# Gate and up products by Strassen's recurrence in a two-layer encoder

## The chip, the core and the metric

The kernel runs on one core of a Trainium2 chip. The metric is the device time of one execution in microseconds (us). The core's engines are TensorE (PE in the rows, its weight loads PEld), VectorE (DVE), ScalarE (ACT), GpSimd (POOL) and SyncE (SP), which issues transfers. Each has a queue of its own and works through it in order; they wait for each other by semaphores. On TensorE the rows give the granted clock as a share of 2.4 GHz.

## The reference

The input is a sequence of 512 tokens of 1024 features, float32. Each of two layers computes, with `rmsnorm(x) = x * rsqrt(mean(x*x) + 1e-6) * gain`:

```
x = x + 0.5 * (silu(h @ w_gate) * (h @ w_up)) @ w_down     h = rmsnorm(x), inner width 2816
p = rmsnorm(x) @ w_in;  A, B, C = three attentions on parts of p
x = x + concat(A, B, C) @ w_out
x = x + 0.5 * (silu(h @ w_gate) * (h @ w_up)) @ w_down     with weights of its own
```

and a last rmsnorm follows. So there are four feed-forward blocks (two per layer) and two mixing stages. The change is in the feed-forward blocks.

## The kernel before

Activations lie transposed: features on the 128 partitions, the 512 tokens along the row. A vector of 1024 features is 8 chunks of [128, 512].

**Products.** Float32 products are made of three products of a rounded format. Each operand is split into a high half, a copy rounded by a cast on ScalarE, and a low half, operand minus high half by one subtraction on VectorE. `mm3` (L450) issues high by high, high by low and low by high, all summed in one PSUM bank. Weights come from memory in float32 (`wr`), and are split in the kernel into `wh` and `wl`; activations are `xgh` and `xgl` (L480).

**A gate/up step.** `ffn` (L673) takes the inner width in two halves of 11 steps, each of 128 inner features. A step is the product of the gate weights (8 chunks of the contraction, so 8 times 3 matmuls of 512 columns) and that of the up weights: 48 matmuls. `gate_steps` (L649) then multiplies by the norm's factor `nm.r`, applies silu, multiplies by the up product and splits the result into `hh` and `hl`. After 11 steps come 8 down products (`dn`) of 33 matmuls each, added to the residual `x` (`down_steps`, L664). There are 4 blocks of 2 halves, so 88 steps.

**Weight stream.** `advance` (L426) loads blocks of 512 KB up to three ahead and splits one ahead, each on three buffers of its own kind (`wraw`, `whi`, `wlo`). All loads are issued by SyncE.

**Residual.** The 8 chunks of `x` stay in the on-chip memory through a feed-forward block; they are stored to DRAM (`xd`) only before a mixing stage, and read back at its output products (`po`).

**The norm.** As chunk m of the new residual is ready, `norm_chunk` (L460) makes `xgh`, `xgl` and the chunk's squares; GpSimd adds the squares up, and two matmuls (`ssq`) and a short chain give `nm.r`. The last chunk's three matmuls of each product are moved to the end of a step, so that the other 42 can run before it is there.

**What sets the order.** The Python code records all operations, and `Recorder.schedule` (L223) lists them by priority (order in the code), readiness by its own costs (`cost`, L152), and free buffers. The result is a fixed order for each engine, with fixed buffers. All operations are issued in L345, so the rows below are told apart by tile names.

Of the kernel before, what the change touches and what calls it, by code (L numbers as in the profile page):

```python
# [18 lines left out]
P = 128  # L19
# [7 lines left out]
HJ = NJ // 2  # L27
EPS = 1e-6
# [105 lines left out]
class Recorder:  # L134
# [17 lines left out]
    def cost(self, eng, what, args, kw, out):  # L152

        n = out.free() if isinstance(out, View) else 1
        psum = any(isinstance(a, View) and a.base.pool == "psum" for a in args[1:])
        if eng == "PE":
            if what == "transpose":
                return 107, 60
            return (n / 2.4) * (4 if args[1].base.dtype == F32 else 1) + 2.5, 60
# [11 lines left out]
        if eng == "POOL":  # L171
            return (120 + 1.08 * n if what == "tensor_scalar" else 145 + 2.11 * n), 60
        return max(650, out.shape[0] * 4 * n / 360), 2000
# [188 lines left out]
class Kern:  # L362
# [18 lines left out]

    def bigt(self, s, shape, dt=F32):
        return self.nc.tile("big", shape, dt, s)
# [24 lines left out]

    def stream(self, blocks):
        self.blocks = blocks  # L410
        self.loaded = {}
        self.halves = {}
        self.nload = self.nsplit = 1
        self.nget = 0
        shape = list(blocks[0].shape)
        t = self.nc.tile("wraw", shape, F32, "wr")
        hi, lo = self.nc.tile("whi", shape, F32R, "wh"), self.nc.tile("wlo", shape, F32R, "wl")
        self.halves[0] = (hi, lo)

        def part(c):  # L420
            self.nc.sync.dma_start(t[:, c], blocks[0][:, c])
            self.nc.scalar.copy(hi[:, c], t[:, c])
            self.nc.vector.tensor_tensor(lo[:, c], t[:, c], hi[:, c].bitcast(F32), ALU.subtract)
        return part

    def advance(self, ahead=1):  # L426
        nc = self.nc
        while self.nload < len(self.blocks) and self.nload < self.nget + 3:
            src = self.blocks[self.nload]
            t = nc.tile("wraw", list(src.shape), F32, "wr")  # L430
            nc.sync.dma_start(t, src)
            self.loaded[self.nload] = t
            self.nload += 1
        while self.nsplit < self.nload and self.nsplit < self.nget + 1 + ahead:
            t = self.loaded.pop(self.nsplit)
            hi = nc.tile("whi", list(t.shape), F32R, "wh")
            lo = nc.tile("wlo", list(t.shape), F32R, "wl")
            nc.scalar.copy(hi, t)
            (nc.gpsimd if self.nsplit in self.slow else nc.vector).tensor_tensor(lo, t, hi.bitcast(F32), ALU.subtract)
            self.halves[self.nsplit] = (hi, lo)  # L440
            self.nsplit += 1

    def weight(self, ahead=1):
        self.advance(ahead)
        w = self.halves.pop(self.nget)
        self.nget += 1
        return w


    def mm3(self, ps, a, b, first, last):  # L450
        mm = self.nc.tensor.matmul
# [8 lines left out]
    def norm_chunk(self, nm, src, gain, last):  # L460
        nc = self.nc
        lo = None
        if gain is not None:
# [23 lines left out]
    def new_norm(self, dim=D, table=False):  # L487
        nm = Kern.Norm()
        nm.xg, nm.acc, nm.r, nm.rc, nm.dim, nm.table = [], None, None, None, dim, table
        return nm  # L490
# [24 lines left out]
    def split_steps(self, src, s, scale=None, eng=None):  # L515
        hi, lo = self.pair(s)
# [26 lines left out]
    def setup(self, blocks):  # L543
        nc, io = self.nc, self.io
        self.x = [self.slot("x") for _ in range(KD)]
# [6 lines left out]
        nm = self.new_norm(table=True)  # L552
        part = self.stream(blocks)
        part(slice(0, 2))
        for k in range(KD):
            nc.sync.dma_start(self.x[k], io["xT"][:, k, :])
            if k == 0:
                nc.sync.dma_start(self.gains, io["gains"])
            self.norm_split(nm, self.x[k], self.gains_cols(G_F1, k))()
            if k == 0:  # L560
                part(slice(2, KD))
        cst = nc.tile("keep", [P, NCONST], F32, "cst")
# [7 lines left out]
        for k in range(KD):  # L570
            self.start(self.norm_chunk(nm, self.x[k], None, k == KD - 1))
# [59 lines left out]
    def ffn_blocks(self, l, f):  # L631
        out = []
        for h in range(2):
            for j in range(HJ):
                for g in range(2):
                    out.append(self.io["wgu"][l, f, h * HJ + j, :, g])
# [12 lines left out]
    def gate_steps(self, nm, pss, hi, lo):  # L649
        nc = self.nc  # L650
        while nm.r is None:
            yield
        t = self.slot("t1")
        nc.vector.tensor_tensor(t, pss[0], nm.r, ALU.mult)
# [3 lines left out]
        nc.vector.tensor_tensor(t, pss[1], t, ALU.mult)  # L658
# [5 lines left out]
    def down_steps(self, nm, m, ps, after):  # L664
# [3 lines left out]
        nc.vector.tensor_tensor(self.x[m], self.x[m], t, ALU.add)  # L668
        yield
        if after:  # L670
            yield from after(m)

    def ffn(self, nm, after, task=None, final=None):  # L673
        for half in range(2):
# [3 lines left out]
            for j in range(HJ):  # L678
                if j == 1 and task and half == 0:
                    self.start(slowly(task, 6))  # L680
                w = [self.weight()]
                pss = [self.ps("gu"), self.ps("gu")]
                self.product(pss[0], w[0], nm.xg, range(KD - 1), 0, KD - 1)
                w.append(self.weight())
                self.product(pss[1], w[1], nm.xg, range(KD - 1), 0, KD - 1)
                for g in range(2):
                    self.product(pss[g], w[g], nm.xg, [KD - 1], 0, KD - 1)
                self.start(self.gate_steps(nm, pss, *h[j]))
            if half == 1:
                nm.xg = None  # L690
            for m in range(KD):
                if final and half == 1 and m == KD - 1:
                    final(h)
# [5 lines left out]
                self.start(self.down_steps(nm, m, ps, after if half == 1 else None))  # L699
# [153 lines left out]
    def mix(self, l, nm, after):  # L853
# [233 lines left out]
        def post(u):  # L1087
# [18 lines left out]
            mixed[k] = yield from self.split_steps(o, "mx", eng=None if kind == "c" else nc.gpsimd)  # L1106
# [81 lines left out]
    def run(self):  # L1188
        nc, g = self.nc, self.gains_cols
        blocks = []  # L1190
        self.slow = set()
        for l in range(DEPTH):
# [6 lines left out]
        def follow(base, table, store=False):  # L1199
            nxt = self.new_norm(table=table)  # L1200

            def after(m):
                if store:
                    nc.sync.dma_start(self.xd[m], self.x[m])
                yield from self.norm_chunk(nxt, self.x[m], None if base is None else g(base, m), m == KD - 1)
                if store:
                    self.x[m] = None
            return nxt, after

        for l in range(DEPTH):  # L1210
            nxt, after = follow(G_MIX + 8 * l, True, True)
            self.ffn(nm, after, self.setup_all() if l == 0 else None)
            nm = nxt
            nxt, after = follow(G_F2 + 8 * l, False)
            self.mix(l, nm, after)
            nm = nxt
            if l + 1 < DEPTH:
                nxt, after = follow(G_F1 + 8 * (l + 1), True)
                self.ffn(nm, after)
# [3 lines left out]
    def finale(self, nm):  # L1223
# [62 lines left out]
        self.ffn(nm, after, final=final)  # L1286
# [5 lines left out]
T = {'offs': (1, 3, 5, 6), 'fill': (3, 3, 3, 2, 2, 2, 1), 'v': 18, 'pairs': (22, 32, 40), 'tl': 1, 'po': 2, 'grp': 2, 'yst': 2, 'pool': (4, 5, 11, 17, 19, 21, 23, 25), 'cstt': 3, 'psc': 0, 'order': (0, 6, 1, 3, 7, 4, 2, 5)}  # L1292
SIZES = {'slots': 57, 'big': 6, 'wraw': 3, 'whi': 3, 'wlo': 3, 'psum': 8, 'small': 24}
# [90 lines left out]
```

## Time and profile before

| | |
|---|---|
| time, median of 3 runs | 2028.42 us (2026.98 to 2028.52) |
| the profiled execution's own time | 2028.95 us, of which the span is 2027.1 us |
| TensorE busy | 1989.6 us (98%) |
| VectorE, ScalarE, GpSimd busy | 1088.9, 819.7, 371.3 us |
| TensorE's granted clock, mean | 0.989 of 2.4 GHz |
| moved by transfers | 231.35 MB, 114 GB/s |

A matmul's end is modelled, and matmuls overlap, so a busy share of TensorE says that it had something in it; its pace is read from the distance of starts. "Idle before" an operation names who released it. "To landing" is from the issue of a transfer to its last byte.

### The profile page before, as it was taken

The page shows a single profiled execution, that of the slowest core. Times are in us where ns is not written, and L with a number is a line of the kernel's source. Part 1 is how long each engine was busy: PE and PEld are TensorE (multiplying, and loading weights), DVE is VectorE, ACT ScalarE, POOL GpSimd, SP SyncE. Part 2 cuts the span into 40 slices and gives each one's busy share as a digit, 9 for nine tenths or more (in the row PEclk, how much of TensorE's full clock was granted, in tenths as well). Part 3 has the DMA queues.
Part 4 walks back from the last instruction along what each step waited for, and adds up shares of the span by engine and source line. Part 5 has one row for each costly group of instructions (what it writes and reads, how often), then busy time and mean ns, then how long its engine had stood idle before and what let it go on. Part 6 is the DMA issues. An engine that isn't in the chain of part 4 may idle for free.

```text
span 2027.1 us, 24516 instructions
## 1 busy us (share of the span) xinstructions
PE 1989.6 (98%) x9119; PEld 1644.0 (81%) x9119; DVE 1088.9 (54%) x1697; ACT 819.7 (40%) x1333; POOL 371.3 (18%) x322
## 2 busy tenths in 40 slices
PE   7999999999899999999999999999989999999997
PEld 5888888887688888888888888888867888888886
DVE  8444444579984434344543444356899744343435
ACT  5222223467784322222332222244668743222333
POOL 4100000146573000000100000012575620000001
PEclk8999999999899999999999999999999999999999
DMA  5434423574532223332323232245743332233222
GB/s 188 139 119 144 136 86 110 161 205 139 129 114 75 92 86 94 104 104 81 107 94 104 86 111 84 91 134 163 227 122 87 99 103 88 87 107 104 95 89 77
DMA packets 90247, 231.35 MB, mean 114 GB/s; under 512 B 12433, under 2 KB 14993, under 8 KB 90129
## 3 DMA queue, kind: packets, MB, share of 16 engines
q1 hardware_dynamic: 90128, 229.79, 36.5%
q8 instruction: 72, 1.18, 0.2%
q14 instruction: 47, 0.38, 0.1%
HBM read 197.24 MB, written 11.53 MB: 103 GB/s over the span
## 4 chain that ended last, share of the span: by engine, by line
PE 87%; DVE 7%; ACT 2%; issue 2%; POOL 1%; DMA 1%; SPq 0%; DVEq 0%; ACTq 0%; POOLq 0%
PE gu L345 47%; PE dn L345 24%; PE po L345 4%; PE pj L345 3%; PE pv L345 3%; PE sc L345 2%; PE av L345 2%; PE tr L345 2%; DVE p L345 1%; PE qn L345 1%; DVE wl L345 1%; ACT p L345 1%; POOL p L345 1%; DVE xgl L345 1%; DVE ptl L345 1%
## 5 line engine op out<-in xcount | busy, mean ns | idle before, releaser
L345 ACT CAST wh<-wr 128x1024 fp32r<-128x1024 f32 (+4 forms) x367 | 339.8, 948 | 857.8 <-PE gu L345 524.2
L345 PE MATMUL gu<-xgh,wh 128*128 128x512 f32 x1408 | 550.5, 391 | 1.7 <-ACT xgh L345 1.7
L345 PE MATMUL gu<-xgl,wh 128*128 128x512 f32 x1408 | 550.7, 391 | 1.1 <-DVE xgl L345 1.0
L345 PE MATMUL gu<-xgh,wl 128*128 128x512 f32 x1408 | 550.3, 391 | 1.2 <-DVE wl L345 1.2
L345 DVE TENSOR_TENSOR wl<-wr,wh 128x1024 fp32r<-128x1024 f32 (+4 forms) x351 | 389.5, 1129 | 139.5 <-ACT wh L345 139.0
L345 PEld LDWEIGHTS gu<-xgl,wh 128*128 128x128 f32 x1408 | 265.6, 189 | 58.1 <-DVE xgl L345 3.0
L345 DVE TENSOR_TENSOR t<-gu,r 128x512 f32<-128x512 f32 x88 | 60.8, 691 | 468.8 <-PE gu L345 468.8
L345 PEld LDWEIGHTS gu<-xgh,wh 128*128 128x128 f32 x1408 | 265.8, 189 | 57.7 <-ACT xgh L345 2.2
L345 PEld LDWEIGHTS gu<-xgh,wl 128*128 128x128 f32 x1408 | 265.6, 189 | 56.7 <-DVE wl L345 1.7
L345 POOL TENSOR_TENSOR sq<-sq,sq 128x512 f32<-128x512 f32 x52 | 79.9, 1536 | 1255.5 <-ACT sq L345 1250.1
L345 PE MATMUL dn<-hl,wh 128*128 128x512 f32 (+2 forms) x715 | 276.2, 386 | 0.0
L345 PE MATMUL dn<-hh,wl 128*128 128x512 f32 (+2 forms) x715 | 276.0, 386 | 0.0
L345 PE MATMUL dn<-hh,wh 128*128 128x512 f32 (+2 forms) x715 | 276.0, 386 | 0.0
L345 PEld LDWEIGHTS dn<-hh,wl 128*128 128x128 f32 x715 | 134.3, 188 | 27.1
L345 PEld LDWEIGHTS dn<-hh,wh 128*128 128x128 f32 x715 | 134.3, 188 | 27.1
L345 PEld LDWEIGHTS dn<-hl,wh 128*128 128x128 f32 x715 | 134.3, 188 | 27.0
L345 POOL TENSOR_SCALAR p<-p,ri 128x512 f32<-128x512 f32 x148 | 114.0, 779 | 95.0 <-DVE ri L345 66.2
L345 DVE SCALAR_TENSOR_TENSOR dt<-dn,r 128x512 f32<-128x512 f32 (+1 forms) x65 | 44.4, 683 | 115.9 <-PE dn L345 115.9
L345 ACT CAST hh<-t 128x512 fp32r<-128x512 f32 x88 | 54.7, 622 | 128.1 <-DVE t L345 128.1
L345 DVE TENSOR_TENSOR hl<-t,hh 128x512 fp32r<-128x512 f32 x88 | 62.0, 704 | 58.5 <-ACT hh L345 58.5
L345 DVE TENSOR_TENSOR ptl<-tr,pth 128x512 fp32r<-128x512 f32 x128 | 86.7, 681 | 8.3 <-ACT pth L345 7.7
L345 PE MATMUL tr<-cst,p 128*128 128x128 f32 x512 | 79.4, 279 | 8.3 <-DVE ptl L345 4.3
(190 smaller groups left out, 2476.5 us busy)
## 6 DMA issues: line engine op xcount, KB each, us to landing
wr<-in_wgu_dram SPq DMA_DIRECT2D x175, 512.0 KB, 3.9
wr<-in_wdn_dram SPq DMA_DIRECT2D x64, 384.0 KB, 3.1
wr<-in_wdn_dram SPq DMA_DIRECT2D x64, 320.0 KB, 3.1
wr<-in_wf_dram SPq DMA_DIRECT2D x26, 512.0 KB, 4.1
bias<-nd SPq DMA_DIRECT2D x32, 256.0 KB, 4.0
bias<-ba SPq DMA_DIRECT2D x32, 256.0 KB, 3.6
wr<-in_wo_dram SPq DMA_DIRECT2D x16, 512.0 KB, 3.7
bi<-in_lncm_dram SPq DMA_DIRECT2D x16, 256.0 KB, 4.6
```

Of the source, the lines that this page charges most:

```text
L345: o.fn(*[real(a) for a in o.args], **{k: real(a) for k, a in o.kw.items()})
```

## The change

**Recurrence.** For a step, the weights are seen as 2x2 blocks: rows are the two halves of the contraction (4 chunks each), columns are gate and up. The activations are 2x2 blocks too: the same halves by left and right 256 tokens. Seven products replace eight, each of 4 chunks by 3 matmuls of 256 columns: 84 matmuls for 48 of 512 columns. This holds for 86 of the 88 steps; the first two steps of the first block stay as they were (`T["plain"] = 2`).

**Sums of weights.** A step's weights come in four pieces. `a` is a block and a sum, `b` a sum and a block, `c` a sum and a block, `d` one sum. The sums in `a` and `c` are made by a load and a second transfer that adds to what lies there (`accum_op`), which GpSimd issues after the load has landed: 2 a step, 172 in all. Those in `b` and `d` are made by VectorE.

**Sums of activations.** `norm_fold` makes the differences `t12` and `t34` of the normed chunks on VectorE and splits them as well.

**Combining.** `gate_up` runs the seven products in three PSUM banks. After four of them a copy on ScalarE or an addition on VectorE must read a bank before TensorE may go on writing it.

**Buffers.** The nine weight buffers become a pool of 13 (`duo`), which also holds some pairs of the mixing stage; the general slots go from 57 to 49. The residual lies in DRAM throughout: `ffn` loads each chunk two down products ahead and stores it after the first half.

```diff
+    def load_piece(self, n):
...
+        if kind == "a":
+            nc.sync.dma_start(t[:, 0], b[0])
+            nc.sync.dma_start(t[:, 1], b[2])
+            nc.gpsimd.dma_start(t[:, 1], b[0], accum_op=ALU.add)
+        elif kind == "b":
+            nc.sync.dma_start(t[:, 1], b[3])
+        else:
+            nc.sync.dma_start(t[:, 0], b[2])
+            nc.gpsimd.dma_start(t[:, 0], b[3], accum_op=ALU.add)
+            nc.sync.dma_start(t[:, 1], b[1])
...
+    def split_piece(self, n):
...
+        if kind == "b":
+            nc.vector.tensor_tensor(t[:, 0], self.raw[n + 1][:, 0], self.raw[n - 1][:, 0], ALU.add)
+        elif kind == "d":
+            t = self.duo("wr", (P, 1, HD, P), F32)
+            nc.vector.tensor_tensor(t[:, 0], self.raw[n - 2][:, 0], self.raw[n - 1][:, 1], ALU.add)
+        hi, lo = self.duo("wh", t.shape), self.duo("wl", t.shape)
+        nc.scalar.copy(hi, t)
+        (nc.gpsimd if kind == "slow" else nc.vector).tensor_tensor(lo, t, hi.bitcast(F32), ALU.subtract)
...
+    def norm_fold(self, nm, src, gain, m):
...
+        nc.vector.scalar_tensor_tensor(t[:, right], g[:, right], -1.0, t[:, left], ALU.mult, ALU.subtract)
+        nc.vector.tensor_tensor(t34[:, left], g[:, right], g1[:, right], ALU.subtract)
+        nc.vector.scalar_tensor_tensor(t34[:, right], t[:, right], -1.0, g[:, left], ALU.mult, ALU.subtract)
+        h2, l2 = fac["T2"]
+        nc.scalar.copy(h2, t[:, right])
+        h, l = self.pair("t34")
+        nc.scalar.copy(h, t34)
...
+    def gate_up(self, nm, hi, lo):
...
+        self.folded(r1, w, 0, nm, "11", True)
+        nc.scalar.copy(s1[:, left], r1[:, left])
+        self.folded(r7, w, 1, nm, "T3", True)
+        nc.scalar.copy(s1[:, right], r7[:, left])
+        w = self.weight()
+        self.folded(r1, w, 0, nm, "T2", False)
+        nc.scalar.copy(s2[:, left], r1[:, left])
+        self.folded(r7, w, 1, nm, "T4", False)
+        nc.vector.tensor_tensor(u[:, left], r7[:, left], s2[:, left], ALU.add)
+        w = self.weight()
+        self.folded(r1, w, 0, nm, "T1", False)
+        nc.vector.tensor_tensor(u[:, right], r1[:, left], s1[:, right], ALU.add)
+        self.folded(r2, w, 1, nm, "21", True)
+        nc.vector.tensor_tensor(t[:, left], r2[:, left], s1[:, left], ALU.add)
+        w = self.weight()
+        self.folded(r1, w, 0, nm, "22", False)
+        self.start(self.gate_steps(nm, r1, t, u, hi, lo))
...
+    def ffn(self, nm, xs, after, task=None, final=None):
...
-                if j == 1 and task and half == 0:
+                if j == 4 and task and half == 0:
                     self.start(slowly(task, 6))
...
+            def load_x(m):
+                if m < KD:
+                    x[m] = self.slot("x")
+                    nc.sync.dma_start(x[m], xs[m])
...
-T = {'offs': (1, 3, 5, 6), 'fill': (3, 3, 3, 2, 2, 2, 1), 'v': 18, 'pairs': (22, 32, 40), 'tl': 1, 'po': 2, 'grp': 2, 'yst': 2, 'pool': (4, 5, 11, 17, 19, 21, 23, 25), 'cstt': 3, 'psc': 0, 'order': (0, 6, 1, 3, 7, 4, 2, 5)}
+T = {'plain': 2, 'load': 6, 'split': 2, 'offs': (1, 3, 5, 6), 'fill': (3, 3, 3, 2, 2, 2, 1), 'v': 18, 'pairs': (22, 32, 40), 'tl': 1, 'po': 2, 'grp': 2, 'yst': 2, 'pool': (4, 5, 11, 17, 19, 21, 23, 25), 'cstt': 3, 'psc': 0, 'order': (0, 6, 1, 3, 7, 4, 2, 5)}
-SIZES = {'slots': 57, 'big': 6, 'wraw': 3, 'whi': 3, 'wlo': 3, 'psum': 8, 'small': 24}
+SIZES = {'slots': 49, 'duo': 13, 'big': 6, 'psum': 8, 'small': 24}
```

**Where the order moves.** Two places, both in the second half of layer 0's second feed-forward block. First TensorE, before: the border of the gate and the up product of one step (`gu_1641` gate, `gu_1642` up).

```order
L345 MATMUL gu_1641_7693<-xgh_1380_5954,wh_1636_7628 128x512
L345 MATMUL gu_1641_7693<-xgl_1381_5966,wh_1636_7628 128x512
L345 MATMUL gu_1641_7693<-xgh_1380_5954,wl_1637_7639 128x512
L345 MATMUL gu_1642_7729<-xgh_1335_5734,wh_1639_7686 128x512 [waits Activation_49]
L345 MATMUL gu_1642_7729<-xgl_1336_5746,wh_1639_7686 128x512
L345 MATMUL gu_1642_7729<-xgh_1335_5734,wl_1640_7698 128x512 [waits DVE_49]
```

TensorE after: the border of the products "T3" (into `gu_2081`) and "T2" (into `gu_2080`, which holds "11" already).

```order
L349 MATMUL gu_2081_10297<-t34h_1664_7520,wh_2075_10118 128x256
L349 MATMUL gu_2081_10297<-t34l_1665_7534,wh_2075_10118 128x256
L349 MATMUL gu_2081_10297<-t34h_1664_7520,wl_2076_10219 128x256
L349 MATMUL gu_2080_10278<-t12h_1572_7125,wh_2078_10250 128x256 [waits Activation_49]
L349 MATMUL gu_2080_10278<-t12l_1573_7134,wh_2078_10250 128x256
L349 MATMUL gu_2080_10278<-t12h_1572_7125,wl_2079_10264 128x256 [waits DVE_49]
```

Before, the waits are for the new weights' halves. After, the wait on ScalarE is also for the copy `s1` out of `gu_2080`, and such a border comes every 12 matmuls. Second ScalarE, before:

```order
L345 CAST wh_1630_7618<-wr_1626_7513 128x1024 [waits DMAHW2_49,PE_49,Activation_49]
L345 CAST wh_1636_7628<-wr_1629_7573 128x1024 [waits DMAHW3_49,PE_49,Activation_49]
L345 ACTIVATE t1_1634_7621<-t1_1634_7621 128x512 [waits DVE_49]
L345 CAST hh_1561_7516<-t1_1634_7621 128x512 [waits DVE_49]
L345 CAST wh_1639_7686<-wr_1635_7583 128x1024 [waits DMAHW4_49,PE_49,Activation_49]
L345 CAST wh_1645_7696<-wr_1638_7641 128x1024 [waits DMAHW5_49,PE_49,Activation_49]
```

ScalarE after, in the step whose "11" and "T3" stand above (`DMASW` is a transfer that GpSimd issued):

```order
L349 CAST wh_2094_10261<-wr_2077_10150 128x1024 [waits DMAHW0_49,DMASW6_49,PE_49]
L349 COPY s1_2083_10300<-gu_2080_10278 128x256 [waits PE_49]
L349 ACTIVATE t1_2067_10275<-t1_2067_10275 128x512 [waits DVE_49]
L349 CAST wh_2107_10316<-wr_2090_10227 128x1024 [waits DMAHW4_49,DMASW7_49,PE_49]
L349 COPY s1_2083_10300<-gu_2081_10297 128x256 [waits PE_49]
L349 CAST wh_2092_10333<-wr_2091_10320 128x512 [waits DVE_49,Activation_49]
L349 COPY s2_2084_10340<-gu_2080_10278 128x256 [waits PE_49]
L349 CAST hh_1939_10081<-t1_2067_10275 128x512 [waits DVE_49]
```

Before, no cast stands in front of anything that TensorE needs within the step. After, the casts of summed pieces stand between the copies that free PSUM for TensorE: the cast `wh_2107` is ahead of the copy of `gu_2081`.

## Rows read from the trace of the kernel before

**Rows 1.** The page's head: span, then busy us, share of the span, instructions.

```profile
span 2027.1 us, 24516 instructions
PE 1989.6 (98%) x9119; PEld 1644.0 (81%) x9119; DVE 1088.9 (54%) x1697; ACT 819.7 (40%) x1333; POOL 371.3 (18%) x322
```

**Rows 2.** Chain that ended last, in order of time: start us, us, what.

```profile
203.45 119.68 PE gu L345 x528
323.13 59.84 PE dn L345 x264
...
1018.87 8.85 PE gu L345 x39
1027.71 0.47 PE ssq L345 x2
```

**Rows 3.** Timeline, TensorE, matmuls of 256 columns: start us, us, operation.

```profile
399.74 0.28 PE L345 MATMUL pv<-wh,xgh 128*128 128x256 f32 x1
...
406.10 0.28 PE L345 MATMUL pv<-wh,xgl 128*128 128x256 f32 x1
```

**Rows 4.** Stretches: busy us and count of PE, PEld, DVE, ACT, POOL; clock; DMA share; GB/s.

```profile
841.00:958.00 117.00, 117.00 (x518) 96.91 (x517) 44.11 (x51) 31.32 (x40) 0.00 (x0) 1.00 0.28 89
383.00:659.00 276.00, 269.02 (x1364) 222.35 (x1363) 218.35 (x448) 183.14 (x370) 146.05 (x131) 0.98 0.46 135
1378.00:1654.00 276.00, 268.33 (x1368) 222.32 (x1367) 218.53 (x449) 183.69 (x371) 146.73 (x131) 0.98 0.46 135
```

**Rows 5.** Groups by shape, VectorE: count, busy us, mean ns, idle before.

```profile
L345 DVE TENSOR_TENSOR wl<-wr,wh 128x1024 fp32r<-128x1024 f32 x209 | 259.2, 1267 | 39.9 <-ACT wh L345 39.4
L345 DVE TENSOR_TENSOR hl<-t,hh 128x512 fp32r<-128x512 f32 x88 | 62.0, 704 | 58.5 <-ACT hh L345 58.5
```

**Rows 6.** Timeline, VectorE, at the start and at the end of a down stage.

```profile
3.82 0.42 DVE L345 TENSOR_TENSOR wl<-wr,wh 128x256 fp32r<-128x256 f32 x1 [2.43 <-ACT wh L345]
18.92 5.42 DVE L345 TENSOR_TENSOR wl<-wr,wh 128x1024 fp32r<-128x1024 f32 x3
...
831.90 0.69 DVE L345 SCALAR_TENSOR_TENSOR dt<-dn,r 128x512 f32<-128x512 f32 x1 [2.04 <-PE dn L345]
832.63 0.69 DVE L345 TENSOR_TENSOR x<-x,dt 128x512 f32<-128x512 f32 x1
833.24 1.22 DVE L345 TENSOR_TENSOR wl<-wr,wh 128x1024 fp32r<-128x1024 f32 x1
```

**Rows 7.** ScalarE: groups by shape, and a 256-column cast from the timeline.

```profile
L345 ACT CAST wh<-wr 128x1024 fp32r<-128x1024 f32 x225 | 229.5, 1050 | 574.2 <-PE gu L345 472.7 <-PE dn L345 47.2 <-issue 36.1
L345 ACT CAST hh<-t 128x512 fp32r<-128x512 f32 x88 | 54.7, 622 | 128.1 <-DVE t L345 128.1
3.38 0.40 ACT L345 CAST wh<-wr 128x256 fp32r<-128x256 f32 x1 [1.37 <-DMA wr<-in_wgu_dram]
```

**Rows 8.** Landing of weight loads at 840:958 (512 KB), 781:839 (mostly 320/384 KB); two issues.

```profile
DMA to landing us min/median/max: 3.2/3.8/5.3
DMA to landing us min/median/max: 2.8/3.1/4.1
x<-xd SPq DMA_DIRECT2D x16, 256.0 KB, 4.5
wr<-in_wf_dram SPq DMA_DIRECT2D x26, 512.0 KB, 4.1
```

**Rows 9.** GpSimd, groups by shape: a two-input operation of 512 columns.

```profile
L345 POOL TENSOR_TENSOR p<-p,p 128x512 f32<-128x512 f32 x20 | 28.0, 1399 | 1.3
```

**Rows 10.** Timeline where the last output product gives the last residual chunk.

```profile
658.93 0.39 PE L345 MATMUL po<-mxh,wl 128*128 128x512 f32 x1
...
659.36 0.69 DVE L345 TENSOR_TENSOR x<-x,po 128x512 f32<-128x512 f32 x1 [2.65 <-PE po L345]
...
660.13 0.72 ACT L345 ACTIVATE xgh<-x,gains 128x512 fp32r<-128x512 f32 x1
```

**Rows 11.** Timeline at the start: what TensorE waits for.

```profile
34.30 0.80 PE L345 MATMUL ssq<-ssl,rep 128*128 128x512 f32 x1 [5.89 <-DVE ssl L345]
```

More of the change, by code (lines that the diff above doesn't have):

```diff
@@ L424, in stream @@
-        return part
-    def advance(self, ahead=1):
[L427 to L432, printed above, removed]
-            self.nload += 1
[L434 to L440, printed above, removed]
+        self.pieces = []
@@ new lines, in stream @@
+        for n, b in enumerate(blocks):
+            if isinstance(b, tuple):
+                b = [b[1][:, i // 2, HD * (i % 2):HD * (i % 2) + HD] for i in range(4)]
+                self.pieces += [(kind, b) for kind in "abcd"]
+            else:
+                self.pieces.append(("slow" if n in self.slow else "", b))
+        self.raw = {}
+        self.halves = {}
+        self.nload = self.nsplit = self.nget = 0
+    def load_piece(self, n):
+        nc = self.nc
+        kind, b = self.pieces[n]
+        if kind in ("", "slow"):
+            t = self.duo("wr", b.shape, F32)
+            nc.sync.dma_start(t, b)
+            return t
+        if kind == "d":
+            return None
+        t = self.duo("wr", (P, 2, HD, P), F32)
+        if kind == "a":
[4 more added lines that the diff above has]
+            nc.sync.dma_start(t[:, 1], b[3])
+        else:
+            nc.sync.dma_start(t[:, 0], b[2])
+            nc.gpsimd.dma_start(t[:, 0], b[3], accum_op=ALU.add)
+            nc.sync.dma_start(t[:, 1], b[1])
+        return t
@@ new lines, in split_piece @@
+    def split_piece(self, n):
+        nc = self.nc
+        kind = self.pieces[n][0]
+        t = self.raw[n]
+        if kind == "b":
[6 more added lines that the diff above has]
+        (nc.gpsimd if kind == "slow" else nc.vector).tensor_tensor(lo, t, hi.bitcast(F32), ALU.subtract)
+        self.halves[n] = (hi, lo)
@@ new lines, in advance @@
+    def advance(self, ahead=1):
+        while self.nload < len(self.pieces) and self.nload < self.nget + T["load"]:
+            self.raw[self.nload] = self.load_piece(self.nload)
+            self.nload += 1
+        fold = self.pieces[min(self.nget, len(self.pieces) - 1)][0] in "abcd" and self.pieces[self.nget][0]
+        while self.nsplit < self.nload and self.nsplit < self.nget + 1 + (T["split"] if fold else ahead):
+            if self.pieces[self.nsplit][0] == "b" and self.nload < self.nsplit + 2:
+                break
+            if self.nsplit not in self.halves:
+                self.split_piece(self.nsplit)
@@ L445, in weight, with mm3 @@
         w = self.halves.pop(self.nget)
+        self.raw.pop(self.nget - 3, None)
         self.nget += 1
         return w
-    def mm3(self, ps, a, b, first, last):
-        mm = self.nc.tensor.matmul
+    def mm3(self, ps, a, b, first, last, **kw):
+        mm = partial(self.nc.tensor.matmul, **kw)
         mm(ps, a[0], b[0], start=first, stop=False)
@@ L462, in norm_chunk @@
         lo = None
-        if gain is not None:
+        if gain is not None and nm.fold:
+            self.start(self.norm_fold(nm, src, gain, nm.n))
+            nm.n += 1
+        elif gain is not None:
             lo = self.norm_split(nm, src, gain)
@@ L570, in setup, with fold @@
         for k in range(KD):
-            self.start(self.norm_chunk(nm, self.x[k], None, k == KD - 1))
+            self.start(self.norm_chunk(nm, x[k], None, k == KD - 1))
+        def fold():
+            for k in (0, 4, 1, 5, 2, 6, 3, 7):
+                yield from self.norm_fold(nm, x[k], self.gains_cols(G_F1, k), k)
+                yield
+        self.start(fold())
         return nm
@@ L634, in ffn_blocks @@
             for j in range(HJ):
-                for g in range(2):
-                    out.append(self.io["wgu"][l, f, h * HJ + j, :, g])
+                w = self.io["wgu"][l, f, h * HJ + j]
+                out += [w[:, 0], w[:, 1]] if (l, f, h) == (0, 0, 0) and j < T["plain"] else [("gu", w)]
             for m in range(KD):
@@ L647, in product, with folded @@
                 self.tick()
-    def gate_steps(self, nm, pss, hi, lo):
-        nc = self.nc
+    def folded(self, ps, w, i, nm, fac, first):
+        for k in range(HD):
+            while fac not in nm.fac.get(k, ()):
+                self.tick()
+            self.mm3(ps[:, 0:HS], (w[0][:, i, k, :], w[1][:, i, k, :]), nm.fac[k][fac],
+                     first and k == 0, k == HD - 1, skip_group_check=not first)
+        self.tick()
+    def gate_up(self, nm, hi, lo):
+        nc = self.nc
+        left, right = slice(0, HS), slice(HS, S)
+        r1, r7, r2 = (self.ps("gu") for _ in range(3))
+        s1, s2, u, t = (self.slot(n) for n in ("s1", "s2", "u", "t1"))
+        w = self.weight()
[13 more added lines that the diff above has]
+        nc.vector.tensor_tensor(t[:, left], r2[:, left], s1[:, left], ALU.add)
+        w = self.weight()
+        self.folded(r1, w, 0, nm, "22", False)
+        self.start(self.gate_steps(nm, r1, t, u, hi, lo))
@@ new lines, in gate_up_plain, with gate_steps @@
+    def gate_up_plain(self, nm, hi, lo):
+        w = [self.weight()]
+        pss = [self.ps("gu"), self.ps("gu")]
+        self.product(pss[0], w[0], nm.plain, range(KD - 1), 0, KD - 1)
+        w.append(self.weight())
+        self.product(pss[1], w[1], nm.plain, range(KD - 1), 0, KD - 1)
+        for g in range(2):
+            self.product(pss[g], w[g], nm.plain, [KD - 1], 0, KD - 1)
+        self.start(self.gate_steps(nm, pss[0], None, pss[1], hi, lo))
+    def gate_steps(self, nm, r1, t, u, hi, lo):
+        nc = self.nc
+        left, right = slice(0, HS), slice(HS, S)
@@ L678, in ffn @@
             for j in range(HJ):
-                if j == 1 and task and half == 0:
+                if j == 4 and task and half == 0:
                     self.start(slowly(task, 6))
[L681 to L688, printed above, removed]
-            if half == 1:
-                nm.xg = None
+                (self.gate_up_plain if nm.plain and half == 0 and j < T["plain"] else self.gate_up)(nm, *h[j])
+            if half == 1:
+                nm.xg = nm.fac = nm.t = nm.plain = None
+                xs = [self.xd[m] for m in range(KD)]
+            x = {}
+            def load_x(m):
+                if m < KD:
+                    x[m] = self.slot("x")
+                    nc.sync.dma_start(x[m], xs[m])
+            load_x(0)
+            load_x(1)
             for m in range(KD):
+                load_x(m + 2)
                 if final and half == 1 and m == KD - 1:
+                    self.x[m] = x[m]
                     final(h)
@@ L698, in ffn @@
                     self.product(ps, w, h, range(6 * c, 6 + 5 * c), 0, HJ - 1, 6 * c)
-                self.start(self.down_steps(nm, m, ps, after if half == 1 else None))
+                self.start(self.down_steps(nm, m, ps, x[m], after if half == 1 else None))
     def scores(self, terms, qc):
@@ L1217, in run @@
             if l + 1 < DEPTH:
-                nxt, after = follow(G_F1 + 8 * (l + 1), True)
-                self.ffn(nm, after)
+                nxt, after = follow(G_F1 + 8 * (l + 1), True, True)
+                self.ffn(nm, xs, after)
                 nm = nxt
```

154 lines of the change are left out of this document (111 added, 43 removed).

## Prediction

> **What bounds the kernel now.** I read the page's head first: TensorE has work in 1989.6 of 2027.1 us, VectorE is at 54%, ScalarE at 40% [rows 1]. The chain of waits says the same by stage: 528 gate/up matmuls run in 119.68 us with no wait between them, 0.2267 us each [rows 2]; behind them 264 down matmuls at the same pace. The table of stretches shows the one other kind of stage: in the two mixing stages TensorE idles 6.98 and 7.67 us in 276 [rows 4]. The reader should see that nothing but fewer TensorE microseconds shortens this kernel, and that in a gate/up stretch the others have much room: of 117 us VectorE works 44.11, ScalarE 31.32, GpSimd nothing, and the transfers take a share of 0.28 [rows 4]. The change spends this room.
>
> **TensorE's saving.** In the timeline of the mixing stage 54 matmuls of 256 columns start between 399.74 and 406.10: 6.36/53 = 0.1200 us each [rows 3], against half of 0.2267 = 0.1134. So a step was 48 x 0.2267 = 10.88 us and becomes 84 x 0.1200 = 10.08. Of the eighth that the recurrence saves (1.36 us) the narrower matmul takes back 84 x 0.0066 = 0.56. 86 steps x 0.80 = **-68.8 us**. The clock stood at 1.00 in the 512-column stretch and at 0.98 in the mixing stage [rows 4], so 0.1200 is no better than full clock.
> The Trainium skill has a rule on this, in "TensorE: Matmul & The Clock Gate", section "Back-to-back issue gap": a single matmul's gap is columns/2.4 plus 2.5 ns, 109 ns for 256 columns. By it the step would save 1.19 us and the change 102. The rows speak against it at both widths: 226.7 is 512/2.4 + 13.4 and 120.0 is 256/2.4 + 13.3 ns.
>
> **VectorE and ScalarE in a step.** VectorE's new list, with durations from rows: three low halves of 1024 columns at 1.22 us (the undisturbed one), one of 512, two weight sums of 512 and one multiplication of 512 at 0.69, the low half `hl` at 0.70, five PSUM or norm operations of 256 columns at 0.42 [rows 5, 6]. That is 3.66 + 2.76 + 0.70 + 2.10 = 9.22 us of a 10.08 us step. Starts in rows 6 lie 0.73 and 0.61 us apart for operations listed at 0.69, so some of it overlaps and I count about 8.2. ScalarE: three casts at 1.05, one at 0.62, three copies at 0.40, silu and `hh` at 0.62 [rows 7]: 6.2 us. Both fit, so neither is a term; VectorE near its limit is a rival.
>
> **Hand-offs inside a step.** Four times a step TensorE writes a bank that a copy or addition must have read (the second product into it comes one product later): 344 times. The cover is one product, 12 x 0.12 = 1.44 us; the needed work is a 256-column operation (0.40 to 0.42) and the way to it and back, but it can stand behind a 1.22 us operation in its queue. The nearest row for such narrow hand-offs is the mixing stage: 7 us idle over at least 128 of them (4 heads' groups of scores and values, counted low), 0.055 us each: 344 x 0.055 = **+19**. Ends: nothing, when the cover always holds; and 0.16 us more each, since a matmul listed at 0.28 and paced at 0.12 [rows 3] can hide that much idleness from a busy sum, +74.
>
> **Accumulated pieces.** Two pieces a step are ready only after a load and then a transfer that GpSimd issues when the load has landed. I counted, in TensorE time by the order, how far the release of a piece's buffer lies ahead of the first operation that TensorE needs and that stands in its queue behind that piece's cast. The example is shown in the order of ScalarE after: `wh_2107` stands ahead of the copy that frees `gu_2081`, which TensorE needs 73 matmuls (8.76 us) after the buffer's last reader; less the cast (1.05) and the hop and copy, 7.3 us are left. Of 172 pieces 36 have this 7.3, 26 have 8.9, the rest 10 or more. The chain L of load and accumulation: a 256 KB load lands in 3.0 us by the mostly 320 and 384 KB loads (median 3.1) and in 4.5 in the mixing stage [rows 8]. An accumulating transfer is in no row. Low: it is a plain load, 2.8. High: it moves its bytes twice, 2 x 3.2, and GpSimd prepares it as long as it takes for a two-input operation, 1.4 [rows 9]: 7.8. I take 3.8, the 512 KB load [rows 8], since it reads as many bytes (source and target) as that. So L = 3.0 + 0.3 of issue + 3.8 = 7.1, and 0.5 more because the step moves 2304 KB (five loads of 256, two accumulations that move 256 twice) for 1024, which takes the share from 0.28 to some 0.68 by my estimate (a 512 KB load took 4.1 for 3.8 where the share was 0.46 [rows 4, 8]). At L = 7.6 the cost is 36 x 0.3 = **+11**. Ends: none at L = 7, and 36 x 5.1 + 26 x 3.5 = 275 at L = 12.4.
>
> **The four starts of a block.** Before, a gate/up stretch begins without a wait (the gap of 0.47 is two `ssq` matmuls [rows 2]), because the last chunk's matmuls go to a step's end. After, the last chunk's factors enter from the second product on. At the first block of the program the first two steps are plain and cover it. At the three others TensorE has some 43 matmuls, 5.16 us, while the last chunk goes through the residual addition (0.69, and 0.43 to reach it), the scaled copy (0.72), three narrow operations, a cast and a low half [rows 6, 7, 10]: 5.6 us, and at two of them the cover is 37 matmuls. Some 1.5 us each, **+4.5**; between 0 and 12, the latter if the eight chunks' extra operations queue up.
> The program's start: TensorE waited 5.89 us for `ssl` [rows 11] behind the angle set-up on VectorE, which moves to step 4. In its place come some 23 operations of 256 columns and a few of 512, 13 us, slower where GpSimd works too (5.42/3 = 1.81 for 1.22 [rows 6]), under 96 plain matmuls, 21.8 us. I take **0**, from -6 to +8.
>
> **The rest.** Residual chunks are loaded two down products (15 us) ahead and land in 4.5 [rows 2, 8]; the stores wait for nobody. The cover is the down stage of 59.84 us; without it, a late chunk delays only VectorE's addition, eight times a half. In the mixing stages the buffers change (49 slots and some pairs in the pool of 13): no row prices that, 0 with 5 us either side.
>
> **Sum.** -68.8 + 19 + 11 + 4.5 = -34.3. The profiled execution took 2028.95, so 1994.6; it lies 0.5 above the median of 2028.42. Forecast: **1994**.
>
> **Rivals.**
> *Late accumulations (slower).* Place: ScalarE's queue, where the cast of a summed piece stands ahead of the copy that frees a bank. At L = 10 the 36 short cases cost 2.7 and the 26 next 1.1 us: 126, in place of 11, so 2109. With the other terms kept, the whole change breaks even at L = 8.6; over that it is slower. For it: 7.1 is a sum of two transfers with one unknown, and the second passes GpSimd. Rows 6 show that VectorE's operations stretch by half with GpSimd beside them, so the two do hold each other up. Against: between transfers GpSimd has nothing to do in a gate/up stretch [rows 4].
> The Trainium skill speaks for this rival, in "SBUF — State Buffer", section "SBUF: two separate sides": transfers issued by GpSimd need it to write descriptors, and a VectorE operation that takes the shared port keeps it out until its end. Which of VectorE's operations here do so no row shows; with VectorE at some 80% a wait of one operation (1.2 us) would bring L to 8.8, the late pieces to 54 us and the sum to +9.
> *No stalls.* If the cover of one product and of the loads holds everywhere, -68.8 and 4.5 are left: 1965. For it: the needed operation takes 0.42 of the cover's 1.44 us. Against: the mixing stage, with its order made by the same code, loses 2.5%.
> *VectorE sets the pace.* If nothing overlaps and each of its 13 operations costs 0.1 us of start besides, a step takes 9.22 + 1.3 = 10.5 us; 86 x (10.88 - 10.5) = 33 saved, 15.5 back for late pieces and starts: 2012. Against: in rows 6 queued operations follow within 0.04 us or overlap.
> *Matmuls of 256 columns go faster than in the mixing stage* (the rule above): by it -102 + 19 + 11 + 4.5, so 1961. The rows leave little for it.
>
> **How the numbers follow.** Chances: the forecast 0.42, late accumulations 0.25, no stalls 0.19, VectorE 0.12, faster matmuls 0.02. The forecast's own range is 1978 to 2018: hand-offs from 4 to 35, late pieces from 0 to 20. About 0.2%, 4 us, is what a measurement of this kernel can tell from no change. Faster takes no stalls, faster matmuls, VectorE, nearly all of the forecast, and none of the late ones: 0.71; within 4 us: 0.06, from the edges of the forecast and of the late accumulations; slower 0.23. The range reaches down to a little under no stalls, 1962, and up to 2065, where the late accumulations (L = 9.3) have half their chance above it.
>
> **What would show it.** In the timeline, gate/up matmuls of 256 columns 0.120 us apart and a half of 11 steps in 111 us plus its gaps. In the waits of TensorE, gaps on `gu` released by ScalarE's `s1`, `s2` and by VectorE's `u`: some 30 us in all; if they are released by a cast or low half of `wh`/`wl`, or the copies themselves start late behind a cast that waits for GpSimd's transfer, the late pieces decide, and the landing of GpSimd's transfers says at what L. VectorE's busy share in these stretches near 0.82; above 0.95 with TensorE waiting for it, the third rival. At the starts of blocks, gaps of 1 to 2 us. Wrong would be a pace off 0.120, gaps of the hand-offs over 0.2 us each, or a time over 2028.

## The result and the profile after

| | median, us | ratio to before, 95% interval |
|---|---|---|
| before | 2028.43 | |
| the change | 2133.22 (2115.87 to 2134.59) | 1.0499 [1.0444, 1.0553] |

The change is slower by 5%, where a gain, to 1994 us, was forecast. The page's head and the stretches after, to be set beside [rows 1, 2, 4] (the columns are those of [rows 4]; two of the eight gate/up stretches, and the sum of all eight):

```profile
span 2130.0 us, 33555 instructions
PE 1976.8 (93%) x12215; PEld 1776.0 (83%) x12215; DVE 1500.9 (70%) x2497; ACT 1080.5 (51%) x1842; POOL 524.0 (25%) x494
...
210.60:351.83 141.23, 121.11 (x925) 118.61 (x924) 96.33 (x143) 61.62 (x97) 28.40 (x27) 0.94 0.67 184
877.53:1006.07 128.54, 115.45 (x926) 114.02 (x924) 91.42 (x141) 61.39 (x97) 16.39 (x19) 0.97 0.62 168
...
sum 1080.61, PE 958.17 PEld 934.08 DVE 794.33 ACT 537.29 POOL 176.34; mean PE 119.77 PEld 116.76 DVE 99.29 ACT 67.16 POOL 22.04
```

The same sum over the eight stretches of before:

```profile
sum 977.36, PE 967.42 PEld 798.18 DVE 412.39 ACT 294.96 POOL 39.82; mean PE 120.93 PEld 99.77 DVE 51.55 ACT 36.87 POOL 4.98
```

The gate/up stretches alone are 103.25 us longer, which is the whole difference of the spans (102.9); down stages and mixing stages take as long as before. TensorE idles 1080.61 - 958.17 = 122.44 us there, for 9.94 before. The granted clock is 0.94 to 0.97, where seven of the eight had 1.00. Who is waited for (us in total, times, longest):

```profile
PE gu L349 <- ACT s L349: 70.7, 34, 5.1
PE gu L349 <- DVE u L349: 29.2, 21, 3.8
PE gu L349 <- DVE wl L349: 7.8, 6, 2.6
```

The first two look like the hand-offs of a step, but they are 55 waits for 344 hand-offs, and long ones. The chain of waits says why (start, us, what):

```profile
1987.03 17.55 PE gu L349 x144
2004.58 0.02 issue
2004.60 3.13 DMA wr<-in_wgu_dram
2007.72 0.02 issue
2007.75 0.04 POOLq L349
2007.79 0.49 issue
2008.28 4.25 DMA wr<-in_wgu_dram
...
2026.73 3.43 DMA wr<-in_wgu_dram
...
2030.73 6.76 DMA wr<-in_wgu_dram
...
2038.60 0.28 ACT s L349
```

The chain runs through a load, half a microsecond, an accumulating transfer, then (at once in the second piece, behind an operation on `t` in the first) a cast and the copy `s`. L, the time from the issue of the load to the landing of the sum, is 7.9 us in the first of these pieces and 10.8 in the second (2026.73 to 2037.49). One case in the timeline of GpSimd, ScalarE, VectorE and TensorE:

```profile
1843.44 0.86 POOL L349 DMA_DIRECT2D wr<-in_wgu_dram  x1 [5.40 <-DVE wl L349]
...
1845.54 0.63 ACT L349 ACTIVATE t<-t 128x512 f32<-128x512 f32 x1 [0.84 <-DVE t L349]
...
1850.96 1.29 DVE L349 TENSOR_TENSOR wr<-wr,wr 128x512 f32<-128x512 f32 x2 [5.45 <-DMA wr<-in_wgu_dram]
1851.00 1.04 ACT L349 CAST wh<-wr 128x1024 fp32r<-128x1024 f32 x1 [4.83 <-DMA wr<-in_wgu_dram]
1851.95 0.37 ACT L349 COPY s<-gu 128x256 f32<-128x256 f32 x1
1852.37 0.58 PE L349 MATMUL gu<-t34h,wh 128*128 128x256 f32 x1 [5.08 <-ACT s L349]
1852.75 0.42 PE L349 MATMUL gu<-t34l,wh 128*128 128x256 f32 x1
1852.97 0.41 PE L349 MATMUL gu<-t34h,wl 128*128 128x256 f32 x1
1853.18 0.41 PE L349 MATMUL gu<-t34h,wh 128*128 128x256 f32 x1
```

The transfer issued at 1843.44 lands 7.5 us later. ScalarE stands with the cast of that piece at the head of its queue and does nothing for 4.83 us, while the copy behind it has its data. TensorE waits 5.08 us. VectorE stands too, 5.45 us, with two sums of weights at the head of its queue. Going back from TensorE's waits by the trace's releasers, 57 of the 70.7 us on `s` (21 waits) stand behind a cast that waits for a landing, and 18 of the 29.2 on `u` (7 waits) behind a sum on VectorE that does so. Behind the wait of the example matmuls start 0.21 us apart, for 0.120 before it. The stretch there, in the columns of [rows 4], has a granted clock of 0.50, the lower of the two levels (1.2 and 2.4 GHz):

```profile
1852.37:1855.00 2.63, 2.63 (x12) 2.63 (x13) 1.87 (x3) 2.39 (x4) 0.00 (x0) 0.50 0.00 0
```

The landings, median us:

```profile
wr<-in_wgu_dram SPq DMA_DIRECT2D x430, 256.0 KB, 3.6
wr<-in_wgu_dram POOLq DMA_DIRECT2D x172, 256.0 KB, 5.0
```

### The profile page after: what moved, and what is told of

Read it like the earlier page. It is cut to its first block, busy times and chain, and to the rows that moved or that the text cites. A ratio compares the mean times of both kernels' runs of the same rounds, so it can differ in the third digit from the quotient of the medians.

```text
span 2130.0 us, 33555 instructions
## 1 busy us (share of the span) xinstructions
PE 1976.8 (93%) x12215; PEld 1776.0 (83%) x12215; DVE 1500.9 (70%) x2497; ACT 1080.5 (51%) x1842; POOL 524.0 (25%) x494
## 5 line engine op out<-in xcount | busy, mean ns | idle before, releaser
L349 ACT CAST wh<-wr 128x1024 fp32r<-128x1024 f32 (+5 forms) x539 | 486.1, 911 | 623.5 <-PE gu L349 136.3
L349 DVE TENSOR_TENSOR wl<-wr,wh 128x1024 fp32r<-128x1024 f32 (+5 forms) x523 | 563.5, 1082 | 234.3 <-PE dn L349 122.0
L349 PE MATMUL gu<-t34h,wh 128*128 128x256 f32 x688 | 204.9, 298 | 53.9 <-ACT s L349 53.9
L349 PE MATMUL gu<-t12h,wh 128*128 128x256 f32 x688 | 203.4, 296 | 20.5 <-ACT s L349 16.9
L349 PE MATMUL gu<-t34l,wh 128*128 128x256 f32 x688 | 202.2, 294 | 0.1
L349 PE MATMUL gu<-t34h,wl 128*128 128x256 f32 x688 | 201.9, 293 | 0.0
L349 PE MATMUL gu<-t12l,wh 128*128 128x256 f32 x688 | 200.4, 291 | 0.0
L349 PE MATMUL gu<-t12h,wl 128*128 128x256 f32 x688 | 199.7, 290 | 0.5 <-DVE wl L349 0.5
L349 PE MATMUL gu<-vh,wh 128*128 128x256 f32 x528 | 152.5, 289 | 14.8 <-DVE u L349 13.0
L349 ACT COPY s<-gu 128x256 f32<-128x256 f32 x258 | 94.9, 369 | 130.8 <-PE gu L349 130.4
L349 PE MATMUL gu<-vl,wh 128*128 128x256 f32 x528 | 151.4, 287 | 0.7 <-DVE vl L349 0.7
```

The costliest lines, as they stand in the source:

```text
L349: o.fn(*[real(a) for a in o.args], **{k: real(a) for k, a in o.kw.items()})
```

## Experiments

The theory tested here is that summed pieces are late, and that the order makes this costly. The order is laid out with costs of the code's own (`cost`): 0.73 us plus 2.0 for such a load and 1.0 + 3.0 for an accumulating transfer, so it takes a summed piece for ready after 6.7 us and puts its cast there. In the trace it is ready after some 9.6. The rivals are the hand-offs as such, VectorE's pace, the narrower matmuls pulling the clock down, and too few buffers.

**Without the accumulating transfers** (e1).

```diff
     def issue(self):
...
+            if "accum_op" in o.kw:
+                continue
```

> The changed kernel with its order of instructions as it is, but the 172 accumulating transfers are not issued, so the sums in pieces a and c hold one term only. Theory (late pieces): a piece is ready about 9.5 us after its load is issued (4.0 load + 0.6 + 5.0 accumulation) instead of the 7.6 of the prediction, the casts that wait for it stand ahead of the copies that free PSUM, and the stalls also lower the granted clock. Without the second transfer the chain is 4 us: TensorE's idle time in the eight gate/up stretches falls from 122 to 20 to 40 us, the clock there from 0.94-0.97 to 0.98 or more, time 1970 to 2000. Rival (hand-offs): the copies are late because of the 1 us operations ahead of them, not because of transfers: idle stays over 90 us, time over 2080. Rival (VectorE's pace): all of its operations are still there, time over 2060. Rival (clock by the narrow matmuls themselves): idle falls, but the clock in the stretches stays at 0.94-0.97, time about 2030.

The time is 1973.91 us, ratio 0.9739 [0.9724, 0.9753]. The stretches:

```profile
818.08:928.92 110.84, 110.84 (x925) 110.83 (x924) 90.99 (x141) 61.45 (x97) 0.00 (x0) 1.00 0.45 150
...
sum 923.56, PE 906.84 PEld 891.73 DVE 788.83 ACT 536.93 POOL 51.43; mean PE 113.36 PEld 111.47 DVE 98.60 ACT 67.12 POOL 6.43
```

TensorE idles 923.56 - 906.84 = 16.72 us, less than the 20 to 40 expected; the clock is 0.97 in the first stretch and 0.99 to 1.00 in the others, and three of the four second halves take 110.84 us without any wait. The traces show the same order on TensorE, ScalarE and VectorE as in the change, so the loss comes from the transfers. Hand-offs, VectorE and a clock pulled down by narrow matmuls themselves fall as causes.

**The order's costs corrected** (e2; e5 corrects only the first line, e6 only the second).

```diff
             if what == "dma_start":
-                return 1000, 3000
+                return 900, 5600
...
-        return max(650, out.shape[0] * 4 * n / 360), 2000
+        return max(650, out.shape[0] * 4 * n / 360), 3300
```

> The changed kernel with two of the order's costs corrected to what the trace shows (landing of a load 3.3 us behind its issue time for 2.0, of an accumulating transfer 5.6 for 3.0): same operations, transfers and buffers, another order. Late pieces as a matter of order (a waiting cast ahead of ready copies): the copies move ahead of the casts, idle in gate/up 30 to 60 us, time 1985 to 2030. Late pieces as a matter of too few buffers (13) for a chain of 9.5 us: the order cannot help, time 2090 to 2130. Hand-offs rival: no change of more than 20 us.

> The changed kernel, with only the accumulating transfer's cost in the order corrected (0.9 + 5.6 us for 1.0 + 3.0); loads stay at 2.0 behind their issue. The order then reckons with 9.15 us for a summed piece, against 9.5 measured. If the whole chain's length is what counts: most of the gain of e2, 1995 to 2020, the mixing stages as before the correction (274 us, for 277 in e2). If single loads being late (pieces b and d, and the 512 KB loads) matter as well: 2020 to 2060.

> The changed kernel, with only the loads' cost corrected (3.3 us for 2.0); the accumulating transfer stays at 1.0 + 3.0. The order reckons with 7.95 us for a summed piece, 1.5 short of the measured 9.5 (before: 6.65, 2.9 short). Chain's length: about half of the gain of e2, 2045 to 2090. If the mis-costed loads alone were the cause: below 2010.

| the order takes L for | kernel | median, us | ratio, interval |
|---|---|---|---|
| 6.7 us | the change | 2133.22 | 1.0499 [1.0444, 1.0553] |
| 8.0 | e6 | 2040.84 | 1.0061 [1.0034, 1.0087] |
| 9.2 | e5 | 2011.32 | 0.9926 [0.9902, 0.9950] |
| 10.5 | e2 | 1994.48 | 0.9845 [0.9821, 0.9870] |

The landings in e2, then its stretches, then ScalarE at a border of a step:

```profile
wr<-in_wgu_dram SPq DMA_DIRECT2D x430, 256.0 KB, 3.7
wr<-in_wgu_dram POOLq DMA_DIRECT2D x172, 256.0 KB, 4.8
```

```profile
sum 939.25, PE 912.85 PEld 896.84 DVE 794.08 ACT 551.74 POOL 169.74; mean PE 114.11 PEld 112.11 DVE 99.26 ACT 68.97 POOL 21.22
```

```profile
1851.43 0.37 ACT L349 COPY s<-gu 128x256 f32<-128x256 f32 x1 [0.36 <-PE gu L349]
1851.83 0.62 ACT L349 CAST hh<-t 128x512 fp32r<-128x512 f32 x1
1852.48 0.62 ACT L349 CAST wh<-wr 128x512 fp32r<-128x512 f32 x1
1853.01 0.36 ACT L349 COPY s<-gu 128x256 f32<-128x256 f32 x1
1854.19 1.05 ACT L349 CAST wh<-wr 128x1024 fp32r<-128x1024 f32 x1 [0.81 <-PE gu L349]
```

The operations, transfers and buffers are the same and the chain is about as long as in the change; idle time is 26.40 us for 122.44 (30 to 60 was expected) and the time 139 us less. In these lines the copies stand ahead of the cast of 1024 columns. A cast can still wait for a landing, but less. In the change and in e2:

```profile
ACT wh L349 <- DMA wr<-in_wgu_dram: 124.8, 42, 7.7
```

```profile
ACT wh L349 <- DMA wr<-in_wgu_dram: 49.8, 22, 9.8
```

So thirteen buffers are enough, and the loss was one of order. e6 came out a little faster than expected, e5 as expected.

**What adding costs** (e4: the second transfer without `accum_op`).

> The same order; GpSimd's second transfer stays but is a plain load (it overwrites instead of adding, so the sums hold one term). It prices what the adding itself costs. If adding makes the transfer long (5.0 us against some 3.3 for a plain one from GpSimd), L falls to about 7.8 and the time to 2030-2070. If it is GpSimd's way of issuing that is long, the landing stays near 5 us and the time at 2110-2135.

The time is 2048.67 us, ratio 1.0112 [1.0086, 1.0137], as expected for a long addition, with 71.21 us idle. The landings:

```profile
wr<-in_wgu_dram SPq DMA_DIRECT2D x430, 256.0 KB, 3.5
wr<-in_wgu_dram POOLq DMA_DIRECT2D x172, 256.0 KB, 3.7
```

Adding makes it 5.0 for 3.7; that GpSimd issues it costs nearly nothing (3.7 against SyncE's 3.5). A chain shorter by 1.3 us is worth 85 us in an order that is this tight.

**Sums on GpSimd** (e3) **and on VectorE** (e8, with e2's costs).

```diff
-            nc.gpsimd.dma_start(t[:, 1], b[0], accum_op=ALU.add)
+            nc.gpsimd.tensor_tensor(t[:, 1], t[:, 1], t[:, 0], ALU.add)
...
-            nc.gpsimd.dma_start(t[:, 0], b[3], accum_op=ALU.add)
+            nc.gpsimd.tensor_tensor(t[:, 0], t[:, 0], self.raw[n - 1][:, 1], ALU.add)
```

> The two accumulating transfers of a step are replaced by two additions on GpSimd from pieces that lie on the chip already (b0+b2 inside piece a, b2+b3 with b3 from piece b): same sums, 172 transfers fewer. Chain: load 3.5 + GpSimd's addition 1.4 to 1.7 = 5.2 us, under the 7.3. Late pieces: idle in gate/up 20 to 50 us, time 1975 to 2020, unless GpSimd's additions lengthen VectorE's operations (1.22 to 1.8 us each while GpSimd works): then VectorE comes near 10 us a step and the time is 2020 to 2060. Hand-offs rival: over 2080.

> e2 with the accumulating transfers replaced by two more additions on VectorE: chain of one load and 0.69 us, no late pieces, but VectorE's list is 9.22 + 1.38 = 10.6 us for a step of 10.08. VectorE's pace (third rival of the prediction, pushed over the edge): the steps become 10.6, so some 45 us over e2, 2030 to 2045, with VectorE's share in the stretches over 0.95. If queued operations overlap by 0.08 as counted: 9.6 us a step, 1985 to 2000.

e3 takes 2079.88 us, ratio 1.0256 [1.0240, 1.0271]. That is over both ranges expected for late pieces and at the edge of the hand-offs' (over 2080); it does not bring that rival back, since e1 and e2 have the same hand-offs and idle 16.72 and 26.40 us. The groups of weight sums on GpSimd and VectorE in e3, and VectorE's in the change:

```profile
L349 POOL TENSOR_TENSOR wr<-wr,wr 128x512 f32<-128x512 f32 x86 | 133.5, 1553 | 473.5 <-DMA wr<-in_wgu_dram 279.9 <-PE gu L349 70.3 <-DVE t L349 44.4
```

```profile
L349 DVE TENSOR_TENSOR wr<-wr,wr 128x512 f32<-128x512 f32 x172 | 156.3, 929 | 27.4 <-POOL wr L349 18.8 <-PE dn L349 6.4 <-PE gu L349 1.4
```

```profile
L349 DVE TENSOR_TENSOR wr<-wr,wr 128x512 f32<-128x512 f32 x172 | 116.0, 688 | 146.2 <-DMA wr<-in_wgu_dram 137.2 <-PE dn L349 7.5 <-PE gu L349 1.2
```

VectorE's additions take 929 ns for 688 in the change, and the order, made with 1.23 us for GpSimd's and nothing for this, has many short waits (56 on `s`, 2.1 us at most). How much of the 53 us over before is due to either was not separated. e8 takes 2002.41 us, ratio 0.9872 [0.9857, 0.9887], 2 us above the range expected if operations overlap (1985 to 2000) and far under the other. One of its stretches:

```profile
836.84:947.90 111.06, 111.06 (x926) 110.95 (x925) 99.02 (x157) 61.48 (x96) 0.00 (x0) 1.00 0.46 151
```

VectorE, with two additions more per step, has 108.4 us of listed operations in this stretch, is busy 99.02 of 111.06 us, and TensorE never waits. Listed durations overlap, as [rows 6] had it, and within the steps VectorE does not set the pace. At the starts of blocks, where it also makes the norm's factors, it may: two of these stretches take 119.19 and 119.80 us for e2's 115.00 and 114.83, with VectorE busy 94% of them.

**The start** (e7: e2 with `'plain': 3` and the set-up at step 6).

> e2 with three plain steps for two and the angle set-up at step 6 for 4: the first gate/up stretch, 137.3 us in e2 with 13.7 idle, gives VectorE and ScalarE more time for the factors of the norm. Start too crowded: 125 to 132 us there, in all 1980 to 1990. If its waits are those for loads: no change, 1994.

The time is 1982.45 us, ratio 0.9779 [0.9762, 0.9796]; as expected, the first stretch takes 130.8 us for 137.4.

**Later residual loads** (e11: a residual chunk's load is issued where its down product starts).

```diff
+            if who and who[0] == "x" and who[1:] in at:
+                late[who[1:]] = o
+                continue
+            if who and who[0] == "at":
+                order.append(late.pop(who[1:]))
+            order.append(o)
```

> The changed kernel with one move in its issue order: the load of residual chunk m is issued when the down product m starts, and no longer up to 30 us before the down stage; all else in its order. In the trace of the change 28.8 of the 122 us of idle time in gate/up stretches lie 10 to 20 us before their ends, where accumulating transfers landed in 6.6 us (4.9 elsewhere) beside 5 to 8 residual loads. If the residual's loads cause this (the prediction put them at 0): those waits go, idle 90 to 100 us, time 2085 to 2105. If they are only beside it (the down weights' loads and the chain's length do it): 2115 to 2135. A late chunk would delay only VectorE's addition.

The time is 2111.71 us, ratio 1.0409 [1.0390, 1.0428], between the two expectations. The last accumulating transfer of the stretch of the example above, in the change and in e11 (window of that transfer alone):

```profile
DMA to landing us min/median/max: 7.5/7.5/7.5
```

```profile
DMA to landing us min/median/max: 4.0/4.0/4.0
```

In the eight stretches that transfer takes 6.0 to 7.5 us beside four or five residual loads, and 4.0 to 5.1 without. The sum over its stretches shows 105.20 us of idle time for 122.44:

```profile
sum 1055.22, PE 950.02 PEld 925.90 DVE 793.53 ACT 537.48 POOL 181.48; mean PE 118.75 PEld 115.74 DVE 99.19 ACT 67.18 POOL 22.68
```

**Versions faster than before and than the change.** e9 is e8, and e10 e7, with the higher load cost for gate/up pieces only; e12 is e10 with e11's move.

> e8 (all sums of weights on VectorE, no accumulating transfer) with the start of e7 (three plain steps, angles at step 6) and the loads' cost raised to 3.3 us for the gate/up pieces only, so that the order of the mixing stages stays at the shorter one (552 to 555 us for both, 561 in e8). If these parts add up: 2002 - 7 to 12 (start) - 6 to 8 (mixing) = 1982 to 1990. If VectorE, now with some 10 us of listed work in a step of 10.08, loses what the start gains: 1995 to 2005.

> e7 (accumulating transfers, corrected costs, three plain steps) with the loads' cost raised for the gate/up pieces only. The mixing stages go from 557 back to 552 to 555, the gate/up stretches stay: 1976 to 1981. If the down stages' loads needed the higher cost too, the stretches behind them get gaps: 1985 to 2000.

> e10 with the same move. Its order leaves summed pieces time enough, and TensorE idles 2.4 us in that place: 1978 to 1983, no gain of more than 3 us.

They take 1989.74 (0.9818 [0.9802, 0.9834]), 1982.61 (0.9782 [0.9767, 0.9798]) and 1978.18 us (0.9744 [0.9728, 0.9761]); e9 and e12 came as expected, and e10 missed its 1976 to 1981. The mixing stages became shorter in e10 (274 us each for 277), but its second stretch got waits back (119.6 us for e7's 114.5), so nothing was won over e7. e12 is the fastest version with all sums made: 2.6% under before.

## Why the prediction was wrong

**The step that failed** is "Accumulated pieces": L was put at 7.6 us, cost +11. Its parts measured: load 3.6 (taken 3.0), issue 0.5 (0.3, from no row), accumulation 5.0 (3.8 plus 0.5 for the load on the transfers). By the medians L is 9.1, and by the means over the 172 pieces 9.6 (4.0 for the load that landed last, 0.6, 5.0), which the prediction's own count prices at 36 x 2.3 + 26 x 0.7 = 101 us. Measured: idle of the change less idle of e1, 122.44 - 16.72 = 106. That the two agree so well is partly luck: the count has one L for all pieces, where accumulating transfers alone land in 3.5 to 9.0 us. The mechanism, the place (the cast ahead of the copy in ScalarE's queue) and the count stood in the prediction as the rival of late accumulations, at L = 10 and 2109 us, with a chance of 0.25. VectorE's queue, where 18 us of the waits arise, is a second place that it did not name. The nearest row, a plain 512 KB load, was no likeness of a transfer that reads what it writes; with a price that runs from 0 to 275 us within the bounds of one unknown, and a break-even 1 us above the value taken, 0.25 was too little.

**The term that was missing** is the clock. [Rows 4] showed 0.98 in stages with short waits, but no term charged the stalls for it. The starts of the matmuls in the change give its size. From the distance of each start to the next I take the pace at full clock (0.120 us, 0.2267 for 512 columns); what is left is loss by the clock where the granted clock was at the lower level (0.213 us from start to start for 256 columns), and waits elsewhere. Over the eight stretches the clock lost 42.6 us (5.4 before) and the waits 147.5 us (12.5 before): -68.9 of pace, +37 of clock and +135 of waits are the 103.25 us. The idle time in the rows, 122.44 us, misses 25 us of these waits, because a matmul's modelled end covers them. Counted in the same way, e1 has 28.6 us of waits and 4.4 of clock, so the late pieces cost 119 us in waits and 38 in clock, 157 us together, which is the difference of the two sums of stretches. In e1 and in e2's undisturbed stretches the clock is at 1.00, so it was the waits and not the narrower matmuls. Long waits cost more of it than short ones: e3 idles 78 us in 145 waits on gate/up products and loses 12.8 us to the clock, the change 119 us in 77 waits and 42.6.

**Residual.** It was put at 0 because its loads have 15 us. Its own lateness did cost nothing, but its loads are issued up to 30 us early and run beside an accumulating transfer, which then lands 2 to 3 us later. Some 20 us of the change are due to that (2133 to 2112), and little once the order has room (e12 against e10: 4 us by the medians, 2 by the stretches of the two traces).

**What held.** The pace: 110.84 us for an 11-step half without waits, predicted 110.9. Hand-offs, +19, were too dear: in e1 TensorE waits 3.0 us on `s` and 1.6 on `u`. The three starts, +4.5, were too cheap: e1's stretches there last 115.21, 117.49 and 115.21 for 110.84, which is +14 after the 0.5 us that each start had before. The 5.6 us of that term do not come out of the operations it lists either, which add up to some 4. The program's start, 0: e1's first stretch takes 128.68 for 138.08, of which 9 x 0.80 = 7.2 is the pace. Mixing stages: 0, as put. VectorE's pace: refuted by e8 for the steps. With nothing late the whole is 1973.91, between the forecast and the rival "no stalls".

The prediction weighed a rule of the Trainium skill, "SBUF — State Buffer", section "SBUF: two separate sides": while a VectorE operation holds the shared port, GpSimd cannot write descriptors. e4 shows no such delay: GpSimd's plain transfer lands in 3.7 us for 3.5 by SyncE's, with VectorE busy 73% of the span. Whether any of its operations there are of the kind that the rule means, no run shows. The delay was in the adding.

## What to carry to other kernels

Where a program makes the order of each engine from costs of its own, read those costs against the trace before anything else: an operation that is taken for ready too early is put at the head of an in-order queue, and all behind it pays, many times the error (2.9 us in L cost 139 us, and two numbers gave them back). Price an operation that no row shows by what it must do, and where the sum turns within its bounds, let the chance say so. A long stall of TensorE is charged twice, once for itself and once for the clock behind it (here 119 and 38 us).

## Not expected of the hardware

An accumulating transfer of 256 KB from DRAM lands in 5.0 us for 3.7 of a plain one on the same queue, and occupies GpSimd 876 ns for 542. It lands in 6.0 to 7.5 beside four or five residual loads (4.0 to 5.1 without them). An addition of two 128x512 operands takes GpSimd 1.55 us beside a busy VectorE, whose own additions go from 688 to 929 ns. In e8 VectorE took 108.4 us of listed operations in a stretch of 111.06 us without making TensorE wait.
